# Attention's value projection in two pairs of seven block products, feature blocks turned in two portions, and the inverse norm turned behind the values

## The chip, the cores and the metric

The kernel runs on one core of one Trainium2 chip. The metric is the device time of one execution in microseconds (us), as the median of several runs. Engines are named as in the profile: PE is TensorE's matrix multiplication, PEld its loading of the stationary operand, DVE is VectorE, ACT ScalarE, POOL GpSimd, SP SyncE, which issues most DMAs. L181 means line 181 of the kernel before.

## What is computed

A two-layer decoder trunk on 256 tokens with 2048 features, all in 32-bit floats. Layer 0 mixes by two recurrent groups and layer 1 by attention; each layer ends in an MLP with 8192 hidden features. What the change touches is layer 1's projection and what stands beside it:

```python
def rms_norm(x, gain):
    xf = x.astype(F32)
    y = xf * lax.rsqrt(jnp.mean(xf * xf, axis=-1, keepdims=True) + NORM_EPS)
    return (y * gain.astype(F32)).astype(x.dtype)
...
def dilated_attention(h, positions, w_qkv, w_o):
    qkv = (h @ w_qkv).astype(F32).reshape(bsz, seq, 3, ATTN_HEADS, HEAD_DIM)
    q = partial_rope(qkv[:, :, 0], positions) * (HEAD_DIM ** -0.5)
    k = partial_rope(qkv[:, :, 1], positions)
    v = qkv[:, :, 2]
...
    out = (num / den).reshape(bsz, seq, D_MODEL).astype(h.dtype)
    return out @ w_o
...
def squared_relu_mlp(h, w1, w2):
    return jnp.square(jax.nn.relu(h @ w1)) @ w2
```

There are 16 heads of 128 features; rotary position coding turns the first 32 features of each query and key, by the sine and cosine of position times frequency.

## The kernel before

**Products.** Each 32-bit operand is split into a high part (rounded) and a low part (the rest), and a product is three matmuls: high by high, high by low, low by high. The activations lie in `bufa` (normalised input, turned to features by tokens) and `bufb` (attention's or the MLP's inner result), with high parts in the first 256 columns of each of 16 feature blocks and low parts in the next 256. The residual stream lies in `xall`/`xres` (two token blocks of 128 by 2048 features).

**Weights** stream from memory in units of 128x2048 (1 MB). `units` (L64, L80 to L88) is the list of all of them in order of use. `unit` (L170) hands out the next and calls `fetch` (L108), which runs some two units ahead: a DMA from SP into `raw`, then `split` makes the high part on ACT (L102) and the low part on DVE (L103). There are three buffers of each. Queries, keys and plain values are split in two steps of 1024 columns.

**Seven products for eight.** The MLP's weights go in pairs: two groups of 512 output columns (n0 and n0 + 1) by 16 feature blocks, of which the first eight (four and four, in the order of PAIRED) are paired: two token blocks by two halves of the paired features by two column groups are eight block products of 12 matmuls, and are got from seven, on sums of operands. `combine` (L124) makes the weights' sums: two adds of 128x2048 on DVE (L130) and an accumulating DMA on POOL (L142, into t1), and a third sum by DVE or, for the matrices in T4_DMA (L965), by a second POOL DMA (L148). Those of the activations are the forms in `formx` and `formh`: `combos` and `part_forms` (L591 to L600). `blocks` (L648) runs one pair in the order of ORDERS (L961 to L964), for w2: a, t1, n7, t2, c, n6, t3, d, n2, t4, n3, where n are the plain units of the other eight feature blocks. Four PSUM banks serve: beta for a, t2, t3, t4 and the sum (0, 1), alpha for t1, c and (1, 0), gamma for d and (0, 0), delta for (1, 1); the numbers are column group and token block. A plain unit n6 or n7 works on token block 1 first (into delta), then on token block 0 (into alpha). A bank that is used again must have been read out: `events` say by what, after each product, and `final` after each sum.

**Order on the engines.** Matmuls and turns made through `mm` (L180) and `turn` (L183) keep the order of the program on PE. For the other engines a scheduler orders instructions when the program is built, by priorities: `stream()` and `urgent()` raise those of the weights' stream and of the short work on results. That order is fixed in the built program; each engine works through its own in turn.

**Around the change.** The last MLP of layer 0 ends with `second` (L750): its `to_x` (L754) adds each finished bank to the residual on DVE, and `Norm.add` squares it on ACT with the sum kept (L291). When a feature block of 512 is complete, `to_features` (L614) queues its turning: four turns of 128x128 into PSUM, twice (L184), then the gain and the split into `bufa` (ACT L235, DVE L236). The queue is emptied by `flush` (L188), eight turns in one go. After that, `rstd` (L310) makes the inverse root of the mean square on DVE: one reduction (L295), one scaling (L296), and eleven operations on 128x2 (L317 to L322, three Newton steps), and `over_tokens` (L304) turns it to lie along tokens for the queries and keys (nr, L848). Since attention's input in `bufa` isn't yet divided by the root, values are multiplied by it when they leave PSUM (L348, ACT), and queries and keys after their product. `rotary` (L817) makes sine and cosine: a small DMA of the positions from POOL, some 16 operations of 32x256 on DVE, two Sin on ACT.

Attention goes in four groups of heads (L892 to L907): values of four heads (512 columns, 16 feature blocks, 96 matmuls of 128x512 per token block pair), then for each head `scores` (query and key projection, rope, softmax, turning) and `mix` (L885, weights by values, split into `bufb`). The last group has its values behind its scores. Then w_o's projection (`out_project`, L639) with residual, norm and turning, and the MLP of layer 1.

Of the kernel before, what the change touches and what calls it, by code (L numbers as in the profile page):

```python
# [20 lines left out]
P = 128  # L21
# [20 lines left out]
def trunk_kernel(ctx, tc, x, xtok, cols, tab, masks, pos, fin, w_in, w_gate, w_out, w_qkv, w_o, w1, w2, out):  # L42
# [28 lines left out]
    def plan2(src, i):  # L71
        for what, u in ORDERS[src is w2]:
            units.append((src, None if u is None else i + u, what, i))
# [7 lines left out]
    for layer in range(2):  # L81
        if layer:
            units.extend((w_qkv, i) for i in (0, 1, 3, 2, *range(4, 48)))
            plan(w_o, 16)
        for q in range(4):
            for src in (w1, w2):
                for n in range(0, 4, 2):
                    plan2(src, layer * 64 + q * 16 + 4 * n)  # L88
# [35 lines left out]
    def combine(u, src, i, what, i0):  # L124
# [7 lines left out]
        if what == "a":  # L132
            load("t1", i0 + 4, pair)
            load("a", i)
            held["s"] = pair.tile([P, 2048], F32, name="s")
            add("s", "a", "t1")
        elif what in ("n", "d"):
            load(what, i)
# [5 lines left out]
        if ahead == ("t4",) and src not in T4_DMA(w1, w2):  # L144
            add("s", "s", "d")
        made[u] = Weights(held[{"t1": "s", "t2": "s", "t3": "t1", "t4": "s"}.get(what, what)])
        if what == "c" and src in T4_DMA(w1, w2):
            nc.gpsimd.dma_start(held["s"], src[i0 + 1], accum_op=OP.add)  # L148
# [37 lines left out]
    later = []  # L186

    def flush(due=None):  # L188
        todo = later[:due]
        del later[:due]  # L190
        for f in todo:
            f()

# [110 lines left out]
    def over_tokens(r):  # L304
        p = psc.tile([P, 512], F32, name="pt", bufs=1)
        for j in range(2):
            T.transpose(p[:, j * P:j * P + P], r[:, j:j + 1].to_broadcast([P, P]), ident)
        return p[:, :S]
# [15 lines left out]
    def tokens(src, i0, mov, kgs=(0, 1, 2, 3), by_k=False):  # L324
        ks = PAIRED if src is w2 else range(KB)
        ps = [pmm.tile([P, 512], F32, name="p") for _ in range(2)]
        for g in kgs:
# [12 lines left out]
            flush()  # L340
# [10 lines left out]
    def project(src, i, mov, acc=None):  # L351
# [3 lines left out]
        if later:  # L355
            cross(p, w, jobs[:8], "h")
            flush()
            cross(p, w, jobs[8:12], "h")
            cross(p, w, jobs[:12], "l")
            jobs = jobs[12:]  # L360
# [226 lines left out]
    def open_pairs(layer):  # L587
        pool_ = pairs.enter_context(tc.tile_pool(name=f"pair{layer}", bufs=1))
        return pool_, [pool_.tile([P, 4, 2, 512], F32R, name=n) for n in ("formx", "formh")]
# [12 lines left out]
    pair, (formx, formh) = open_pairs(0)  # L602
# [11 lines left out]
    def to_features(n, gname, forms=None):  # L614
        def work():
            with urgent():
                for half in range(2):
                    p = psc.tile([P, 2, S], F32, name="pl", bufs=2)
                    for j in range(2):
                        for i in range(2):  # L620
                            k = 4 * n + 2 * half + i
                            turn(p[:, i, j * P:j * P + P], xres[:, j, k * P:k * P + P])
                    k = 4 * n + 2 * half
                    if forms is None:
                        for i in range(2):
# [22 lines left out]
    def blocks(src, i0, n0, mov, forms, events, final, soon=False):  # L648
# [6 lines left out]
        beta = psc.tile([P, 512], F32, name="po" if n0 else "pd", bufs=1)  # L655
# [55 lines left out]
    def first(i0, n0, soon):  # L711
# [23 lines left out]
        def final(n, j, bank):  # L735
            with urgent():
# [5 lines left out]
                else:  # L742
# [5 lines left out]
                                             "t3": u3}, final, soon)  # L748
# [24 lines left out]
    def mlp(layer, nrm, nxt, gname):  # L773
# [9 lines left out]
        r2n = tmp.tile([P, 2], F32, name="r2n", bufs=2)  # L783
# [3 lines left out]
        for q in range(4):  # L787
            ends = nxt if q == 3 else None

            def done(n):  # L790
                if ends is None:
                    return
                if gname:
                    to_features(n, gname)
# [6 lines left out]
            for n in (0, 2):  # L801
                first(layer * 64 + q * 16, n, q + n == 0)
# [43 lines left out]
    rt = rstd(nx1)  # L846
    rs = tmp.tile([P, S], F32, name="nr", bufs=1)
    A.copy(rs, over_tokens(rt))  # L848
# [9 lines left out]
    def scores(u0):  # L858
# [9 lines left out]
        s = wk.tile([P, 384], F32, name="as", bufs=3)  # L868
# [12 lines left out]
        st = wk.tile([P, 384], F32, name="pT", bufs=5)  # L881
# [3 lines left out]
    def mix(hd, st, vg, bank="po", bufs=1):  # L885
        vs = slice((hd % 4) * P, (hd % 4) * P + P)
# [78 lines left out]
T4_DMA = lambda w1, w2: (w1,)  # L965
# [32 lines left out]
def _layout(a):  # L998
# [30 lines left out]
    q_, k_, v_ = feat(wq[:, :2048]), feat(wq[:, 2048:4096]), toks(wq[:, 4096:])  # L1029
    w_qkv = []  # L1030
    for g in range(4):
        if g < 3:
            w_qkv.append(v_[4 * g:4 * g + 4])
        for h in range(4 * g, 4 * g + 4):
            w_qkv += [q_[h:h + 1], k_[h:h + 1]]
    w_qkv.append(v_[12:])
# [33 lines left out]
```

## Time and profile before

| what | value |
|---|---|
| median of 3 runs | 2167.29 us (2167.05 to 2167.54) |
| the profiled execution | 2166.9 us |
| its span in the profile | 2165.1 us |
| granted TensorE clock, mean | 0.998 |
| instructions in the profile | 27716 |
| weight splits: high 128x1024 and 128x2048, ACT (L102), in all | 486 + 96 operations, 689.3 + 183.7 us |
| DVE adds of weights 128x2048 (L130) `s<-s,raw` | 48, mean 2282 ns |
| weights by DMA from POOL into t (L142) | 32, median 8.7 us from issue to landing |

The span is the stretch that the profiler sees; what lies around it is 1.8 us. "Busy" of an engine is the time in which it had an instruction running; "idle before" is the time an engine waited ahead of an instruction, with what ended the wait. A chain line gives the start, the length and the instructions of a stretch that set the end.

### The profile page before, as it was taken

How to read it: one execution, taken by the hardware profiler on the slowest of the kernel's cores; microseconds unless marked ns; L12 is line 12 of the kernel's file. 1: busy time of each engine (PE TensorE's matmuls, PEld its weight loads, DVE VectorE, ACT ScalarE, POOL GpSimd, SP SyncE). 2: the span in 40 equal slices, each digit the busy share in tenths (PEclk: the TensorE clock that was granted, in tenths of full speed). 3: DMA queues.
4: the chain of work that ended last, by engine and by line, in shares of the span. 5: the costliest groups of instructions: out<-in, count | busy, mean ns of one | idle time of the engine just before them, and what ended most of it. 6: DMA issues, size and time to landing. Idle time of an engine off the chain costs nothing.

```text
span 2165.1 us, 27716 instructions
## 1 busy us (share of the span) xinstructions
PE 2146.9 (99%) x11044; PEld 1833.8 (85%) x11044; DVE 1792.2 (83%) x2094; ACT 1254.1 (58%) x1413; POOL 44.7 (2%) x57
## 2 busy tenths in 40 slices
PE   9999999999999999999999999999999999999997
PEld 8999998888888888888788888888888888888886
DVE  7776787789889889889877768667998998898897
ACT  7444485566466566466554544456655755755764
POOL 0000000000000000000000000000000000000000
PEclk9999999999999999999999999999999999999999
DMA  8444445587777687687664554557768777777873
GB/s 319 156 156 164 150 157 212 182 244 246 227 237 257 222 247 235 233 252 233 201 208 166 185 172 161 192 181 227 236 221 261 237 227 238 251 233 224 264 239 129
DMA packets 65857, 464.68 MB, mean 215 GB/s; under 512 B 7344, under 2 KB 8112, under 8 KB 10304
## 3 DMA queue, kind: packets, MB, share of 16 engines
q1 hardware_dynamic: 58176, 410.89, 53.2%
q0 software_dynamic: 7264, 51.42, 12.8%
q8 instruction: 87, 1.43, 0.3%
q10 hardware_dynamic: 288, 0.61, 0.1%
q14 instruction: 42, 0.34, 0.0%
HBM read 460.78 MB, written 2.10 MB: 214 GB/s over the span
## 4 chain that ended last, share of the span: by engine, by line
PE 95%; DVE 2%; ACT 1%; DMA 1%; issue 1%; SPq 0%; DVEq 0%; ACTq 0%
PE p L181 67%; PE po L181 12%; PE pd L181 11%; PE pl L184 2%; DVE lo L103 1%; PE pl L476 1%; ACT hi L102 0%; DMA raw<-in_w 0%; PE pl L867 0%; PE po L888 0%; DVE xall L754 0%; DMA xall<-in_x 0%; PE pd L880 0%; PE pd L460 0%; PE pl L866 0%
## 5 line engine op out<-in xcount | busy, mean ns | idle before, releaser
L102 ACT CAST hi<-raw 128x1024 fp32r<-128x1024 f32 (+2 forms) x486 | 689.3, 1443 | 563.0 <-PE p L181 372.7
L103 DVE TENSOR_TENSOR lo<-raw,hi 128x1024 fp32r<-128x1024 f32 (+2 forms) x486 | 822.2, 1708 | 223.1 <-ACT hi L102 205.4
L181 PE MATMUL p<-hi,bufb 128*128 128x512 f32 x1408 | 448.6, 390 | 2.1 <-DVE xall L754 2.0
L181 PE MATMUL p<-hi,bufa 128*128 128x512 f32 x1280 | 411.4, 392 | 0.8 <-ACT hi L102 0.8
L181 PE MATMUL p<-bufa,hi 128*128 128x256 f32 (+1 forms) x1792 | 364.9, 317 | 0.1
L181 PEld LDWEIGHTS p<-hi,bufb 128*128 128x128 f32 x1408 | 264.3, 188 | 60.1 <-DVE xall L754 5.5
L181 PEld LDWEIGHTS p<-bufa,hi 128*128 128x128 f32 x1792 | 294.5, 190 | 18.9 <-DVE hz L418 0.3
L181 PEld LDWEIGHTS p<-hi,bufa 128*128 128x128 f32 x1280 | 240.4, 188 | 53.0 <-DVE y L718 2.4
L181 PE MATMUL p<-lo,bufb 128*128 128x512 f32 x704 | 274.2, 389 | 1.2 <-DVE lo L103 1.2
L181 PE MATMUL p<-bufa,lo 128*128 128x256 f32 x1152 | 255.5, 287 | 0.0
L181 PE MATMUL p<-lo,bufa 128*128 128x512 f32 x640 | 250.6, 392 | 2.2 <-DVE lo L103 2.1
L103 DVE TENSOR_TENSOR lo<-s,hi 128x2048 fp32r<-128x2048 f32 x96 | 219.4, 2285 | 18.4 <-ACT hi L102 16.5
L102 ACT CAST hi<-s 128x2048 fp32r<-128x2048 f32 x96 | 183.7, 1913 | 48.3 <-PE po L181 21.8
L181 PEld LDWEIGHTS p<-bufa,lo 128*128 128x128 f32 x1152 | 189.3, 191 | 2.6
L181 PEld LDWEIGHTS p<-lo,bufb 128*128 128x128 f32 x704 | 132.2, 188 | 28.4 <-DVE lo L103 1.6
L181 PEld LDWEIGHTS p<-lo,bufa 128*128 128x128 f32 x640 | 120.2, 188 | 28.1 <-DVE lo L103 4.3
L130 DVE TENSOR_TENSOR s<-s,raw 128x2048 f32<-128x2048 f32 x48 | 109.5, 2282 | 1.3 <-DMA raw<-in_w 1.3
L181 PE MATMUL po<-hi,bufa 128*128 128x512 f32 x256 | 84.8, 392 | 0.0
L181 PE MATMUL pd<-hi,bufa 128*128 128x512 f32 x256 | 84.8, 392 | 0.0
L181 PE MATMUL p<-hi,formx 128*128 128x512 f32 x256 | 84.0, 389 | 0.0
L181 PE MATMUL p<-hi,formh 128*128 128x512 f32 x256 | 84.0, 389 | 0.0
L181 PE MATMUL pd<-hi,bufb 128*128 128x512 f32 x256 | 83.0, 389 | 0.0
(281 smaller groups left out, 2754.9 us busy)
## 6 DMA issues: line engine op xcount, KB each, us to landing
raw<-in_w SPq DMA_DIRECT2D x224, 1024.0 KB, 5.1
raw<-in_w_qkv SPq DMA_DIRECT2D x48, 1024.0 KB, 4.8
raw<-in_w_in SPq DMA_DIRECT2D x46, 1024.0 KB, 4.9
t<-in_w SPq DMA_DIRECT2D x32, 1024.0 KB, 5.7
t<-in_w POOLq DMA_DIRECT2D x32, 1024.0 KB, 8.7
raw<-in_w_out SPq DMA_DIRECT2D x16, 1024.0 KB, 4.9
s<-in_w POOLq DMA_DIRECT2D x16, 1024.0 KB, 9.2
raw<-in_w_o SPq DMA_DIRECT2D x16, 1024.0 KB, 4.8
```

Of the source, the lines that this page charges most:

```text
L102: A.copy(h, w)
L103: V.tensor_tensor(l, w, h.bitcast(F32), OP.subtract)
L130: V.tensor_tensor(held[to], held[x], held[y], OP.add)
L181: chain[:] = [after(T.matmul(*args, **kw), chain)]
L184: chain[:] = [after(T.transpose(out_, in_, ident), chain)]
L476: T.matmul(pl[:, j], kq[:, js], halves(qp[:, js], c, True), start=True, stop=True)
```

## The change

Attention's values are projected in two pairs of 1024 columns (heads 0 to 7, heads 8 to 15), each by `blocks`, as the MLP's products are, and so on forms of the normalised input in feature blocks 0 to 7; the weights are laid out for it. Each pair's results leave PSUM through `put` (ACT, scaled by the root or its negative) and `add` (DVE, scaled and added). All of `rstd` comes ahead of the first pair, the turning of the root along tokens behind it (now in PE's written order), and `rotary` behind that. Heads go in the order: values of 0 to 7, heads 0 to 7, scores of heads 8 to 11, values of 8 to 15, mix of 8 to 11, heads 12 to 15.

A feature block is now turned in two portions of four turns, each from the list `turns`, one behind a unit; this holds for all three places where blocks are turned (after layer 0's mixers, after layer 0's MLP, after w_o). The buffers change too: `formx`, t1 and s move to a pool that stays for the whole program, so `values` can use them; the pair pool of layer 0's MLP ends before attention and attention's tiles take its room; rotary's tiles move into attention's pool (positions and angle share `ra` and `rb` with rope), vg has one buffer in place of two (each twice as large), as two for three, pT four for five, r2n one for two.

```diff
     def plan2(src, i):
-        for what, u in ORDERS[src is w2]:
+        for what, u in ORDERS[src is not w1]:
             units.append((src, None if u is None else i + u, what, i))
...
-            units.extend((w_qkv, i) for i in (0, 1, 3, 2, *range(4, 48)))
+            for v, heads in ((0, 24), (32, 8)):
+                plan2(w_qkv, v)
+                units.extend((w_qkv, v + 8 + i) for i in range(heads))
             plan(w_o, 16)
...
         if what == "a":
-            load("t1", i0 + 4, pair)
+            load("t1", i0 + 4, both)
             load("a", i)
-            held["s"] = pair.tile([P, 2048], F32, name="s")
+            held["s"] = both.tile([P, 2048], F32, name="s")
             add("s", "a", "t1")
...
             load("c", i0 + 5)
             nc.gpsimd.dma_start(held["t1"], src[i0 + 5], accum_op=OP.add)
             add("s", "s", "c")
-        if ahead == ("t4",) and src not in T4_DMA(w1, w2):
+        if ahead == ("t4",) and src not in T4_DMA(w1, w2, w_qkv):
             add("s", "s", "d")
         made[u] = Weights(held[{"t1": "s", "t2": "s", "t3": "t1", "t4": "s"}.get(what, what)])
-        if what == "c" and src in T4_DMA(w1, w2):
+        if what == "c" and src in T4_DMA(w1, w2, w_qkv):
             nc.gpsimd.dma_start(held["s"], src[i0 + 1], accum_op=OP.add)
...
-    later = []
...
+    def turn_one():
+        if turns:
+            turns.pop(0)()
...
-        ks = PAIRED if src is w2 else range(KB)
+        ks = range(KB)
...
-            flush()
+            turn_one()
...
-        if later:
-            cross(p, w, jobs[:8], "h")
-            flush()
-            cross(p, w, jobs[8:12], "h")
-            cross(p, w, jobs[:12], "l")
-            jobs = jobs[12:]
...
-        return pool_, [pool_.tile([P, 4, 2, 512], F32R, name=n) for n in ("formx", "formh")]
+        return pool_, pool_.tile([P, 4, 2, 512], F32R, name="formh")
...
-    pair, (formx, formh) = open_pairs(0)
+    both = ctx.enter_context(tc.tile_pool(name="both", bufs=1))
+    formx = both.tile([P, 4, 2, 512], F32R, name="formx")
+    pair, formh = open_pairs(0)
...
-        def work():
+        def work(half):
+            k = 4 * n + 2 * half
             with urgent():
-                for half in range(2):
-                    p = psc.tile([P, 2, S], F32, name="pl", bufs=2)
-                    for j in range(2):
-                        for i in range(2):
-                            k = 4 * n + 2 * half + i
-                            turn(p[:, i, j * P:j * P + P], xres[:, j, k * P:k * P + P])
-                    k = 4 * n + 2 * half
-                    if forms is None:
-                        for i in range(2):
-                            split_to(bufa[:, k + i], p[:, i], col(gname, k + i))
-                        continue
-                    z = pair.tile([P, 2, 2, P], F32, name="y21")
+                p = psc.tile([P, 2, S], F32, name="pl", bufs=2)
+                for j in range(2):
                     for i in range(2):
-                        A.activation(z[:, i], p[:, i].rearrange("p (j c) -> p j c", j=2), AF.Copy,
-                                     scale=col(gname, k + i))
-                    zs = z.rearrange("p i j c -> p i (j c)")
-                    split_to(bufa[:, k:k + 2], zs)
-                    a11, a21, a12, a22 = (z[:, i, j] for i in range(2) for j in range(2))
-                    combos(a22, a11, a21, a12, a11, a21, a12, a22)
-                    part_forms(forms, k // 2, 1, slice(0, 4), z.rearrange("p i j (one c) -> p one (i j) c", one=1))
-        later.append(work)
+                        turn(p[:, i, j * P:j * P + P], xres[:, j, (k + i) * P:(k + i) * P + P])
+                if forms is None:
+                    for i in range(2):
+                        split_to(bufa[:, k + i], p[:, i], col(gname, k + i))
+                    return
+                z = pair.tile([P, 2, 2, P], F32, name="y4" if half else "y21")
+                for i in range(2):
+                    A.activation(z[:, i], p[:, i].rearrange("p (j c) -> p j c", j=2), AF.Copy, scale=col(gname, k + i))
+                split_to(bufa[:, k:k + 2], z.rearrange("p i j c -> p i (j c)"))
+                a11, a21, a12, a22 = (z[:, i, j] for i in range(2) for j in range(2))
+                combos(a22, a11, a21, a12, a11, a21, a12, a22)
+                part_forms(forms, k // 2, 1, slice(0, 4), z.rearrange("p i j (one c) -> p one (i j) c", one=1))
+        turns.extend([lambda: work(0), lambda: work(1)])
...
+        beta = psc.tile([P, 512], F32, name="pt" if src is w_qkv and i0 else "po" if n0 else "pd", bufs=1)
...
-        for what, u in ORDERS[src is w2]:
+        for what, u in ORDERS[src is not w1]:
             w = unit(src, None if u is None else i0 + 4 * n0 + u)
+            due, ready = len(later), len(turns)
             if what != "n":
                 times(bank[what], w, side[what])
                 if what in events:
                     events[what](bank[what])
-                if what == "t1" and soon:
-                    flush()
-                continue
-            n, g = divmod(u, 4)
-            plains[n] += 1
-            due = len(later)
-            for j in (1, 0) if n else (0, 1):
-                times(sums[n, j], w, lambda i, j=j, g=g: plain(j, 4 * g + i))
-                if plains[n] == 2:
-                    final(n, j, sums[n, j])
-            flush(due)
+            else:
+                n, g = divmod(u, 4)
+                plains[n] += 1
+                for j in (1, 0) if n else (0, 1):
+                    times(sums[n, j], w, lambda i, j=j, g=g: plain(j, 4 * g + i))
+                    if plains[n] == 2:
+                        final(n, j, sums[n, j])
+                flush(due)
+            if ready:
+                turn_one()
 
...
-                    to_features(n, gname)
+                    to_features(n, gname, formx if n < 2 else None)
...
-    vgs = mixers.enter_context(tc.tile_pool(name="vgs1", bufs=2))
+    vgs = mixers.enter_context(tc.tile_pool(name="vgs1", bufs=1))
     wk = mixers.enter_context(tc.tile_pool(name="wk2", bufs=2))
-    rot = mixers.enter_context(tc.tile_pool(name="rot", bufs=1))
     angles = {}
     swap = [(i + 16) % 32 for i in range(32)]
 
     def rotary():
-        ppi = rot.tile([32, S], I32, name="ppi")
+        ppi = wk.tile([32, S], I32, name="ra", bufs=2)
         nc.gpsimd.dma_start(ppi, bass.AP(tensor=pos.tensor, offset=pos.offset, ap=[[0, 32], [1, S]]))
-        ang = rot.tile([32, S], F32, name="ang")
-        cosT = rot.tile([32, S], F32, name="cosT")
-        sinT = rot.tile([32, S], F32, name="sinT")
+        ang = wk.tile([32, S], F32, name="rb", bufs=2)
+        cosT = wk.tile([32, S], F32, name="cosT", bufs=1)
+        sinT = wk.tile([32, S], F32, name="sinT", bufs=1)
...
-    rt = rstd(nx1)
-    rs = tmp.tile([P, S], F32, name="nr", bufs=1)
-    A.copy(rs, over_tokens(rt))
...
-        s = wk.tile([P, 384], F32, name="as", bufs=3)
+        s = wk.tile([P, 384], F32, name="as", bufs=2)
...
-        st = wk.tile([P, 384], F32, name="pT", bufs=5)
+        st = wk.tile([P, 384], F32, name="pT", bufs=4)
...
-        vs = slice((hd % 4) * P, (hd % 4) * P + P)
+        vs = slice((hd % 8) * P, (hd % 8) * P + P)
...
-    pend = []
-    for g in range(4):
-        if g < 3:
-            vg = tokens_group(w_qkv, g * 12, rt, kgs=(0, 1, 2, 3) if g else (0, 1, 3, 2))
-        if not g:
-            rotary()
-        for hd in range(4 * g, 4 * g + 4):
-            u0 = g * 12 + (4 if g < 3 else 0) + (hd % 4) * 2
-            st = scores(u0)
-            if g < 3:
-                mix(hd, st, vg)
-            else:
-                pend.append(st)
-    vg = tokens_group(w_qkv, 44, rt)
-    for hd, bank in zip(range(12, 16), (("po", 1), ("pd", 1), ("pl", 2), ("pl", 2))):
-        mix(hd, pend[hd - 12], vg, *bank)
+    with urgent():
+        rt = rstd(nx1)
+        rtn = tmp.tile([P, 2], F32, name="rtn", bufs=1)
+        V.tensor_scalar(rtn, rt, -1.0, None, op0=OP.mult)
+
+    def values(i0):
+        v = vgs.tile([P, 2, 2, 512], F32, name="vg")
+
+        def put(n, j, r=rt):
+            def event(bank):
+                with urgent():
+                    A.activation(v[:, j, n], bank, AF.Copy, scale=r[:, j:j + 1])
+            return event
+
+        def add(n, j, bank, r=rt):
+            with urgent():
+                V.scalar_tensor_tensor(v[:, j, n], bank, r[:, j:j + 1], v[:, j, n], op0=OP.mult, op1=OP.add)
+
+        blocks(w_qkv, i0, 0, bufa, formx,
+               {"a": put(0, 0), "t1": put(1, 1), "t2": put(1, 0, rtn), "t3": lambda b: add(1, 1, b, rtn)},
+               lambda n, j, b: put(n, j)(b) if (n, j) == (0, 1) else add(n, j, b))
+        return v.rearrange("p j n c -> p j (n c)")
+
+    vg = values(0)
+    rs = tmp.tile([P, S], F32, name="nr", bufs=1)
+    with urgent():
+        A.copy(rs, over_tokens(rt, turn))
+    rotary()
+    for hd in range(8):
+        mix(hd, scores(8 + 2 * hd), vg)
+    pend = [scores(24 + 2 * i) for i in range(4)]
+    vg = values(32)
+    for i, bank in enumerate((("po", 1), ("pd", 1), ("pl", 2), ("pl", 2))):
+        mix(8 + i, pend[i], vg, *bank)
+    for i in range(4):
+        mix(12 + i, scores(40 + 2 * i), vg)
 
     mixers.close()
-    pair, (formx, formh) = open_pairs(1)
+    pair, formh = open_pairs(1)
...
-T4_DMA = lambda w1, w2: (w1,)
+T4_DMA = lambda w1, w2, w_qkv: (w1, w_qkv)
```

Here `both` is the lasting pool. The weights' layout on the host follows the new order of units, with the values' feature blocks in the order of PAIRED.

More of the change, by code (lines that the diff above doesn't have):

```diff
@@ L184, in turn @@
         chain[:] = [after(T.transpose(out_, in_, ident), chain)]
-    later = []
+    later, turns = [], []
     def flush(due=None):
@@ L302, in inv_mean, with over_tokens @@
             return m
-    def over_tokens(r):
+    def over_tokens(r, turn=lambda o, i: T.transpose(o, i, ident)):
         p = psc.tile([P, 512], F32, name="pt", bufs=1)
         for j in range(2):
-            T.transpose(p[:, j * P:j * P + P], r[:, j:j + 1].to_broadcast([P, P]), ident)
+            turn(p[:, j * P:j * P + P], r[:, j:j + 1].to_broadcast([P, P]))
         return p[:, :S]
@@ L646, in trunk_kernel, with blocks @@
     nrm = out_project(w_out, "nmlp0", (2, 3, 0, 1))
-    def blocks(src, i0, n0, mov, forms, events, final, soon=False):
+    def blocks(src, i0, n0, mov, forms, events, final):
         plain = lambda j, k: (mov[:, k, j * P:j * P + P], mov[:, k, S + j * P:S + j * P + P])
@@ L654, in blocks @@
         alpha, delta, gamma = (pmm.tile([P, 512], F32, name="p") for _ in range(3))
-        beta = psc.tile([P, 512], F32, name="po" if n0 else "pd", bufs=1)
+        beta = psc.tile([P, 512], F32, name="pt" if src is w_qkv and i0 else "po" if n0 else "pd", bufs=1)
         bank = {"a": beta, "t1": alpha, "t2": beta, "c": alpha, "t3": beta, "d": gamma, "t4": beta}
@@ L709, in to_h, with first @@
         later.append(work)
-    def first(i0, n0, soon):
+    def first(i0, n0):
         keep, tiles = {}, {}
@@ L747, in first @@
         blocks(w1, i0, n0, bufa, formx, {"a": hold("y1", A.copy, 2), "t1": hold("y4", V.tensor_copy), "t2": hold("y2", A.copy),
-                                             "t3": u3}, final, soon)
+                                             "t3": u3}, final)
     def second(i0, n0, nrm, r2, r2n, done, gains):
@@ L782, in mlp @@
         r2 = nrm.inv_mean()
-        r2n = tmp.tile([P, 2], F32, name="r2n", bufs=2)
+        r2n = tmp.tile([P, 2], F32, name="r2n", bufs=1)
         V.tensor_scalar(r2n, r2, -1.0, None, op0=OP.mult)
@@ L801, in mlp @@
             for n in (0, 2):
-                first(layer * 64 + q * 16, n, q + n == 0)
+                first(layer * 64 + q * 16, n)
             for n in (0, 2):
@@ L1028, in _layout @@
     wq = n(a["attn_w_qkv"][0])
[L1029 to L1036, printed above, removed]
+    q_, k_, v_ = feat(wq[:, :2048]), feat(wq[:, 2048:4096]), toks(wq[:, 4096:], PAIRED)
+    qk = [w[h:h + 1] for h in range(16) for w in (q_, k_)]
+    w_qkv = [v_[:8], *qk[:24], v_[8:], *qk[24:]]
     w1 = np.concatenate([toks(n(w)[:, q * 2048:q * 2048 + 2048], PAIRED) for w in a["mlp_w1"] for q in range(4)])
```

## The prediction

> **What bounds the kernel now.** I read the page's busy times first, then its chain of work that ended last, then the waits of PE alone, then the timelines of PE and DVE where the first layer's MLP hands over to attention (1050 to 1118 us), because that is where the change puts its work.
>
> ```profile
> PE 2146.9 (99%) x11044; PEld 1833.8 (85%) x11044; DVE 1792.2 (83%) x2094; ACT 1254.1 (58%) x1413; POOL 44.7 (2%) x57
> ...
> PE 95%; DVE 2%; ACT 1%; DMA 1%; issue 1%; SPq 0%; DVEq 0%; ACTq 0%
> ```
>
> PE is the bound nearly everywhere: busy 99% of the span, and 95% of the chain. So a matmul taken away is worth its pace, unless a new wait gives it back. All waits of PE, by what ended them (us in total, times, longest):
>
> ```profile
> PE p L181 <- DVE lo L103: 3.3, 4, 1.2
> PE p L181 <- DVE xall L754: 2.0, 2, 1.3
> PE po L246 <- DVE xp L528: 1.1, 1, 1.1
> ```
>
> Few and short; none is in attention. The pace of a 128x512 matmul is read from the chain, where the 96 matmuls of one values group stand as one line (start, us):
>
> ```profile
> 1422.03 21.78 PE p L181 x96
> ```
>
> 21.78 / 96 = 0.2269 us each (a single record shows 0.39 us, since records overlap). Two of the waits are in the last w2 block of layer 0, and after the second come eight turns of a feature block in one go (start, us, what ran, and in brackets what it had waited for):
>
> ```profile
> 1062.64 0.50 PE L181 MATMUL p<-lo,bufb 128*128 128x512 f32 x1 [1.17 <-DVE lo L103]
> ...
> 1066.17 0.50 PE L181 MATMUL p<-hi,bufb 128*128 128x512 f32 x1 [0.71 <-DVE xall L754]
> ...
> 1069.02 1.03 PE L184 MATMUL pl<-tab__181,xall 128*128 128x128 f32 x8
> ```
>
> The next matmul starts at 1069.81, so eight turns take 0.79 us and four about 0.4. DVE, 83% busy over all, is the late engine here: both waits are for it.
>
> **What goes.** A values pair (1024 columns, 16 feature blocks) is 192 matmuls of 128x512 before and 180 after: 7 block products of 12, and 8 plain ones of 12 for the half of the inputs that is not paired. In order, the built programs differ by exactly 24 such matmuls on PE; turns and all else are as many. 24 x 0.2269 = **-5.45 us**. DVE and ACT get 11 weight splits for 8 in each pair, two adds of 128x2048 (2.28 us each by L130's row), and the forms of feature blocks 0 to 7; SP gets no more than its 1 MB loads, POOL four accumulating DMAs. Inside the values that is hidden: a pair is 180 x 0.2269 = 40.8 us of PE against 11 splits (lo 128x2048: 2.285 us) + 2 adds = 29.7 us of DVE. Most of it is beside PE, except in four places.
>
> **Place 1: the first values block.** Call E the end of the last w2 matmul. PE then runs product a (12 matmuls, 2.72 us), four turns, t1 (2.72), four turns, and the plain unit n7. The last to_x, 0.74 us behind an add of 2.28 us on DVE, is done about E + 2.9; the four turns after a need it, so a PE wait of 0.2 there, and n7's half for token block 1 ends at 2.72 + 0.2 + 0.4 + 2.72 + 0.4 + 2.72, about E + 9.1. Its other half accumulates into the bank that t1 wrote and that the change now evacuates through put(1,1), ACT, scaled by the inverse root of the mean square. Before, values were left in PSUM for 96 matmuls (21.8 us) before anything wanted that root. So the question is when the root is ready. Before, the chain ran like this on DVE (from the reduction of the squares to the last of eleven small operations):
>
> ```profile
> 1105.10 0.14 DVE L295 TENSOR_REDUCE nm<-ss 128x2 f32<-128x8 f32 x1
> 1105.21 0.28 DVE L838 TENSOR_SCALAR cosT<-cosT 32x256 f32<-32x256 f32 x1
> ...
> 1107.50 1.23 DVE L103 TENSOR_TENSOR lo<-raw,hi 128x1024 fp32r<-128x1024 f32 x1 [0.42 <-ACT hi L102]
> 1108.65 0.15 DVE L321 SCALAR_TENSOR_TENSOR rs<-rs,nm 128x2 f32<-128x2 f32 x1
> ...
> 1111.74 0.15 DVE L322 SCALAR_TENSOR_TENSOR nr<-rs,nr 128x2 f32<-128x2 f32 x1
> ```
>
> 6.8 us, mixed with rotary operations and splits, with nobody waiting. In the changed program's DVE order the same chain stands behind the last to_x so: position cast (0.27), lo split of n7 (2.2 start to start), a rotary step (0.25), lo split of t2 (2.2), reduce, one gain split (0.4), a rotary step, mean (together 1.0): E + 8.9. Then lo split of c (2.2): E + 11.1. Then eleven small operations left for the root, with fourteen others among them: three gain splits (0.40 start to start), four rotary 32x256 SCALAR_TENSOR_TENSOR (0.33), seven shorter ones (0.21); the small ones follow at 0.08 to 0.2, 0.12 in the mean. That is 1.2 + 1.3 + 1.5 + 1.3 = 5.3 us, root at E + 16.4. On ACT the Sin table load (1.28 by its row) and two Sin stand ahead of put; they wait for cosT and sinT, that come among the last of these DVE operations; then put(0,0) and put(1,1), 0.69 each by the 128x512 row of L348: about E + 17.7. PE wait: 17.7 - 9.1 = **+8.6 us**. What is queued behind the waiting matmul is all of PE. From below: with the small operations wholly within the others' time, 8.6 - 1.3 = 7.3. From above: the position cast waits for a DMA which POOL issues behind the accumulation of t1, and these took 8.7 us to land in the page's row; up to 2.4 more, 11.
>
> **Place 2: the last w2 block of layer 0.** Turns of block 0 now come in two portions, the first behind product a. They need the to_x of the block before, that stands behind an add which waited for its DMA (1057.44, 1.30 us of waiting); it is done some 5 us after this block's start, against 2.7 for a: a wait of 2.0, and 0.5 later at the turn of block 3. They take the place of the 2.2 us seen above (1.17 + 0.71 and their after-effects). Net **+0.3**; from -1 (the old stalls go and the new ones are smaller) to +2 (DVE has 5.6 us of form work more here and falls further back).
>
> **Place 3: the second values block.** The same half of n7 waits for put(1,1), which stands on ACT behind an exponential of the last pending head, a few tenths to 1.2 us: **+0.6** (0 to 1.2).
>
> **Place 4: before the output projection.** in the built order the two matmuls of mix(15) stand among w_o's, right ahead of the 81st, the first that reads head 15. Nothing is between them to cover mix's split into bufb: a copy on ACT that stands behind two hi splits, then a subtraction on DVE behind lo splits. Its two operations alone take 0.37 and 0.42 us (the 128x256 rows of L232 and L233); a split of 128x2048 in the way, up to 1.9 or 2.3, would cover all but a part of itself. I take **+1.15** (0.6 to 2). Before, the four mixes had w_o's first 80 matmuls, 18 us, behind them.
>
> Turning by fours costs nothing by itself: the change of kind on PE was 0 to 0.1 us in the rows around 1069.
>
> **Sum**, against the profiled execution (2166.9 us, span 2165.1): -5.45 + 8.6 + 0.3 + 0.6 + 1.15 = +5.2, so 2172.1. The median of the runs is 2167.29, 0.4 above that execution: **2172.5 us**.
>
> **The clock.** The 24 warm-up matmuls at the start (L246) show two paces in their records: the first ones 421 ns long and 0.213 us apart until 4.3 us into the span, the later ones 275 ns and 0.112 apart. The half pace cost 15 x 0.101 = 1.5 us. Waits up to 1.5 us later in the kernel left the pace at once as it was. A wait of 8.6 us lies between: nothing to 1.5 us. The profile's granted clock is 1.00 even in the first 4 us, so that row cannot tell. I put nothing in the forecast and 1.5 in a rival. [...]
>
> **Rivals.** (a) *The clock falls in the wait.* Then 2172.5 + 1.5 = 2174.0. For it: the start of the span. Against it: no wait so far did it, but none was over 1.5 us. (b) *DVE falls behind further*: the cast waits for its DMA, and the form operations of four more halves (each four of 128x128 at 0.21 and two of 128x512 at 0.6, by the rows of the same lines in layer 0, less the gain splits that they replace) delay to_x; 2172.5 + 2.4 + 1.7 = 2176.6. For it: DVE already ends both waits there; against it: ACT and the buffers limit DVE too, and DVE idles 1 us here and there before 1092. (c) *The root is in time*: not slower. If the root's operations run as soon as the last square is there (E + 3.7; thirteen operations of 0.2 us: E + 6.3; the two puts done at E + 7.7), the first half of n7 covers it and place 1 costs nothing: 2172.5 - 8.6 = 2163.9, and 2161.9 if places 2 to 4 cost nothing too. It decides at E + 9.1. For it: the edit marks these operations as urgent. Against: they stand in the built order behind three splits of 2.2 us, which cannot be overtaken on one engine. (d) That the change leaves out what it says is excluded: the matmuls are counted.
>
> **Chances.** Forecast 0.45, (a) 0.27, (b) 0.13, (c) 0.11, something else 0.04. Faster or slower counts from 0.2% = 4.3 us, about what a measurement of this kernel can tell: under 2163.0, over 2171.6. The forecast's own low end (7.3, -1 and 0.6 in place of 8.6, 0.3 and 1.15) is 2169.4, so a quarter of it is "same"; (a) is slower but for a tenth, (b) slower, (c) half faster and half same. Faster 0.06, same 0.20, slower 0.74. The range of eight in ten: from 2168.5 (the low end less a little, without (c)) to 2177.5 (upper part of (b)).
>
> **What would show it.** PE's waits: one of 7 to 11 us at a matmul with bufa about 9 us after the last w2 matmul, released by ACT's put; the small operations of the root on DVE 11 to 16 us after E; 24 matmuls fewer; two waits of 2.0 and 0.5 for to_x in the last w2 block; about 1 us ahead of w_o's block 15. After the long wait, matmuls 0.45 us apart for 3 us would show (a). Wrong if no wait over 3 us stands there, or if DVE's order on the chip lets the root out earlier.

## The result and the profile after

The changed kernel takes 2175.97 us (median of 6 runs, 2174.42 to 2176.86) against 2167.68 us of the kernel before on the same chip: ratio 1.0038, 95% interval 1.0025 to 1.0051, 8.3 us slower. The profiled execution took 2176.81 us, 9.9 more than the one before; its span is 2174.7 us, 9.6 more. The page's busy times:

```profile
PE 2147.9 (99%) x11020; PEld 1833.0 (84%) x11020; DVE 1821.7 (84%) x2113; ACT 1268.0 (58%) x1411; POOL 48.2 (2%) x61
```

24 matmuls fewer on PE (11020 for 11044), and yet PE is not busy for less time. Its waits say where a part went (us in total, times, longest):

```profile
PE p L183 <- ACT vg L897: 8.3, 1, 8.3
PE pl L186 <- DVE xall L752: 1.9, 1, 1.9
PE p L183 <- DVE lo L105: 1.8, 3, 0.8
PE p L183 <- DVE xall L752: 1.4, 1, 1.4
...
PE p L183 <- ACT bufb L238: 0.5, 1, 0.5
```

The first line is new and the longest wait of the kernel: put (L897) in the first values block. The second is the turn behind product a in the last w2 block of layer 0; the two waits seen there before are gone. The timeline of DVE shows how late the root is. E, the end of the last w2 matmul, is 1103.3 here, as the next block's first matmul starts at 1103.27:

```profile
1109.03 2.27 DVE L105 TENSOR_TENSOR lo<-s,hi 128x2048 fp32r<-128x2048 f32 x1
1111.23 0.14 DVE L301 TENSOR_REDUCE nm<-ss 128x2 f32<-128x8 f32 x1
...
1111.96 2.27 DVE L105 TENSOR_TENSOR lo<-raw,hi 128x2048 fp32r<-128x2048 f32 x1
...
1116.66 0.14 DVE L327 SCALAR_TENSOR_TENSOR rs<-rs,nm 128x2 f32<-128x2 f32 x1
1116.77 0.41 DVE L830 SCALAR_TENSOR_TENSOR rb<-cosT,rb 32x256 f32<-32x256 f32 x1
...
1119.33 0.16 DVE L328 SCALAR_TENSOR_TENSOR nr<-rs,nr 128x2 f32<-128x2 f32 x1
```

The reduction at E + 8.0, the root at E + 16.2, with splits and rotary operations among its own. ACT takes it up within 0.2 us, as its timeline in the same stretch shows (the two puts):

```profile
1119.68 0.66 ACT L897 ACTIVATE vg<-pd,nr 128x512 f32<-128x512 f32 x1
1120.25 0.66 ACT L897 ACTIVATE vg<-p,nr 128x512 f32<-128x512 f32 x1
```

And PE follows; its timeline from the waiting matmul on:

```profile
1120.97 0.80 PE L183 MATMUL p<-hi,bufa 128*128 128x512 f32 x1 [8.29 <-ACT vg L897]
1121.56 0.63 PE L183 MATMUL p<-lo,bufa 128*128 128x512 f32 x1
1121.99 1.06 PE L183 MATMUL p<-hi,bufa 128*128 128x512 f32 x2
1122.84 0.63 PE L183 MATMUL p<-lo,bufa 128*128 128x512 f32 x1
...
1126.67 0.40 PE L183 MATMUL pd<-lo,formx 128*128 128x512 f32 x1
```

Single matmuls are 0.63 us long here for 0.39, and start 0.43 us apart for 0.227, until 1126.67. The table by stretches of time has the granted clock in its fourth column (start:end length, PE busy and matmuls, clock, DMA share, GB/s):

```profile
1058.00:1061.00 3.00, 1.60 (x9) 1.00 0.38 158
1061.00:1062.00 1.00, 0.52 (x3) 0.90 0.00 0
1062.00:1065.00 3.00, 3.00 (x8) 0.50 0.29 35
1065.00:1066.00 1.00, 1.00 (x5) 0.90 0.52 180
...
1116.00:1117.00 1.00, 0.00 (x0) 0.71 0.90 188
1117.00:1126.00 9.00, 5.03 (x12) 0.50 0.49 159
1126.00:1127.00 1.00, 1.00 (x5) 0.67 0.00 0
```

A clock of 0.90 over a microsecond is 0.2 us at half. So it was at half from 1061.8 to 1065.2, after the turn's wait, and from 1116.4 to 1126.7, in and after the long one. The trace's own record of the clock, from which this column is made, has the same four times.

**Account of the 9.6 us**, from the same matmuls in both timelines: +0.8 up to the last w2 block (0.5 of it from the start to 300 us, most of the rest by 530 us; the first product starts at 6.20 for 5.44); +1.7 in the last w2 block (E is 1103.27 for 1100.74); +6.9 from E to the first turn in w_o (1430.4 for 1421.0, less the 2.5 before it); +0.2 after. The 6.9 is -5.45 for 24 matmuls, about +8.4 for the wait with what follows directly, 13 matmuls at half pace (+2.7), +0.9 for mix of head 15 ahead of w_o, and a rest of 0.3.

The 0.5 of the start goes with the clock; that the edit has no part in it is an estimate, from the warm-up matmuls being the same 24. The clock record shows full rate from 4.34 us on before and only from 7.08 in the change, and the 24 warm-up matmuls take 5.49 us there for 4.50. (The column shows 1.00 ahead of the record's first entry too, so it can't tell this.)

### The profile page after: what moved, and what is told of

Same layout as the page of the kernel before. It is cut to its first block, busy times and chain, and to the rows that moved or that the text cites. A ratio compares the mean times of both kernels' runs of the same rounds, so it can differ in the third digit from the quotient of the medians.

```text
span 2174.7 us, 27696 instructions
## 1 busy us (share of the span) xinstructions
PE 2147.9 (99%) x11020; PEld 1833.0 (84%) x11020; DVE 1821.7 (84%) x2113; ACT 1268.0 (58%) x1411; POOL 48.2 (2%) x61
## 5 line engine op out<-in xcount | busy, mean ns | idle before, releaser
L104 ACT CAST hi<-raw 128x2048 fp32r<-128x2048 f32 (+2 forms) x468 | 683.9, 1484 | 571.7 <-PE p L183 369.3
L105 DVE TENSOR_TENSOR lo<-raw,hi 128x2048 fp32r<-128x2048 f32 (+2 forms) x468 | 816.4, 1759 | 209.3 <-ACT hi L104 194.2
L183 PE MATMUL p<-hi,bufa 128*128 128x512 f32 x1136 | 368.2, 393 | 9.1 <-ACT vg L897 8.3
L183 PEld LDWEIGHTS p<-hi,bufa 128*128 128x128 f32 x1136 | 214.7, 189 | 57.0 <-ACT vg L897 8.7
L105 DVE TENSOR_TENSOR lo<-s,hi 128x2048 fp32r<-128x2048 f32 x102 | 233.2, 2286 | 16.9 <-ACT hi L104 14.8
L183 PE MATMUL p<-lo,bufa 128*128 128x512 f32 x568 | 222.8, 392 | 1.8 <-DVE lo L105 1.8
L104 ACT CAST hi<-s 128x2048 fp32r<-128x2048 f32 x102 | 195.1, 1912 | 48.0 <-PE po L183 22.0
L183 PEld LDWEIGHTS p<-lo,bufa 128*128 128x128 f32 x568 | 107.4, 189 | 24.7 <-DVE lo L105 3.1
L183 PE MATMUL p<-hi,formx 128*128 128x512 f32 x288 | 95.6, 392 | 0.0
L105 DVE TENSOR_TENSOR lo<-t,hi 128x2048 fp32r<-128x2048 f32 x34 | 77.8, 2287 | 13.2 <-ACT hi L104 13.2
```

The source lines that it names most:

```text
L104: A.copy(h, w)
L105: V.tensor_tensor(l, w, h.bitcast(F32), OP.subtract)
L183: chain[:] = [after(T.matmul(*args, **kw), chain)]
```

## Experiments

**Values without the root (e1).** The same mathematics, with the root applied where the softmax weights leave PSUM:

```diff
-        A.copy(st, pt)
+        A.activation(st[:, :S], pt[:, :S], AF.Copy, scale=rt[:, 0:1])
+        A.activation(st[:, S:], pt[:, S:], AF.Copy, scale=rt[:, 1:2])
...
-        def put(n, j, r=rt):
+        def put(n, j, r=1.0):
...
-                    A.activation(v[:, j, n], bank, AF.Copy, scale=r[:, j:j + 1])
+                    A.activation(v[:, j, n], bank, AF.Copy, scale=r)
...
-        rtn = tmp.tile([P, 2], F32, name="rtn", bufs=1)
-        V.tensor_scalar(rtn, rt, -1.0, None, op0=OP.mult)
```

> The changed kernel, but values leave PSUM unscaled (puts and adds with 1 and -1), and the inverse root is applied to the softmax weights when they are copied out of PSUM after their turning (two ACT operations a head in place of one); same mathematics. Theory (the wait is for the root alone, and the half pace after it comes from the wait): the 8.3 us wait in the first values block and the 13 matmuls at 0.43 us after it (2.7 us) both go, 11 us less than the changed kernel: some 3 us below the kernel before, 2164.5. Rival (the block itself is too much for DVE, and the wait only moves to a split or a form): a wait of 3 us or more by DVE lo or formx in that block, and a time above 2168.

Measured 2172.33 us, ratio to before 1.0022 (1.0013 to 1.0032). The wait for put is gone, nothing took its place in the values block, and no matmul between 1040 and 1440 us goes at half pace (the mean granted clock is 0.999, for 0.995 in the change); that much is the theory. But the time is 8 us above the forecast, and neither side foresaw where: e1 loses evenly, in both MLPs, which the edit doesn't touch. Two of the groups of matmuls on forms, in e1 (after the name: busy us in all, mean ns of one):

```profile
L183 PE MATMUL p<-lo,formx 128*128 128x512 f32 x144 | 56.9, 395 | 0.0
L183 PE MATMUL po<-hi,formx 128*128 128x512 f32 x128 | 43.4, 400 | 0.0
```

The same two groups in the changed kernel:

```profile
L183 PE MATMUL p<-lo,formx 128*128 128x512 f32 x144 | 56.0, 389 | 0.0
L183 PE MATMUL po<-hi,formx 128*128 128x512 f32 x128 | 42.7, 395 | 0.0
```

In starts it is clearer: matmuls with formx or formh follow each other after 232.7 ns in the mean in e1, 226.9 in the changed kernel (some 1590 of each counted from 425 to 2140 us); those with bufa or bufb after 227 in both. Dropping the little tile rtn had moved the forms by 32 bytes. e9 and e11 follow this up.

**The w2 portions a unit later (e5).**

```diff
-            if ready:
+            if ready and not (src is w2 and what == "a"):
                 turn_one()
```

> The changed kernel, with the portions in the w2 blocks turned behind t1 and n7 and not behind a and t1. Theory (the 1.9 us wait in the last w2 block is for the last add to the residual, which is done 5 us after the block's start, and the half pace after it follows from the wait): that wait and the half pace of 1061.5 to 1065.3 go, 3.5 to 4 us less than the changed kernel, 2172; the wait of the first values block stays at 8 to 8.6 us. Rival (DVE is late by its form work, and the wait only moves to lo splits as before): 1 to 2 us less at most, with waits of 1 us and more for DVE lo in that block.

Measured 2177.25 us, 1.0045 (1.0032 to 1.0059): not faster than the change. Its timeline of PE shows where the waits are now:

```profile
1063.52 0.50 PE L183 MATMUL p<-lo,bufb 128*128 128x512 f32 x1 [0.85 <-DVE lo L105]
1067.25 0.50 PE L183 MATMUL p<-hi,bufb 128*128 128x512 f32 x1 [0.95 <-DVE xall L752]
1107.57 0.69 PE L186 MATMUL pl<-tab__181,xall 128*128 128x128 f32 x2 [2.64 <-DVE xall L752]
1122.95 0.79 PE L183 MATMUL p<-hi,bufa 128*128 128x512 f32 x1 [7.59 <-ACT vg L897]
```

The two waits of the kernel before are back; that much is the rival's mechanism. The new one of 2.6 us, at the turn in the values block, has another cause, which DVE's timeline shows:

```profile
1104.37 0.28 DVE L820 CAST rb<-ra 32x256 f32<-32x256 int32 x1 [2.46 <-DMA ra<-in_pos]
...
1106.78 0.73 DVE L752 SCALAR_TENSOR_TENSOR xall<-po,nm,xall 128x512 f32<-128x512 f32 x1
```

In this built order the position cast stands ahead of the add of weights (between these lines) and of the last to_x (L752), where it stands behind both in the changed kernel. Its DMA, issued by POOL right behind the accumulation of t1, took 8.5 us to land, and DVE stood idle for it 2.46 us. The turn follows that to_x. So e5 moved more than the portions, and it doesn't tell what turning a unit later alone would give.

**Both (e6).** e1 and e5 together.

> Both edits together: values unscaled with the root in the softmax weights, and the portions of the w2 blocks turned one unit later. Theory: both gains add, 15 us less than the changed kernel, about 2161 and 0.3% under the kernel before; no wait of PE over 1 us between 1040 and 1160 us, and the granted clock is 1.00 there. Rival: something else in the first values block is late next (a put on ACT behind hi splits, a form on DVE), a wait of 2 us or more with its half pace, and 2164 or more.

Measured 2176.18 us, 1.0039 (1.0027 to 1.0052), with the forms 32 bytes off as in e1. The wait for put is gone, but three waits for DVE stand as in e5 (0.5, 0.9 and 2.9 us), the last with half pace behind it (the mean granted clock is 0.997, for 0.999 in e1): the rival's figure, though not with a put or a form. As in e5, the cast stands ahead of the last to_x and waits for its DMA, here 2.75 us.

**Turns in portions alone (e3)**: the kernel before with `turn_one`, the two halves of to_features and the loop of `blocks` from the change's diff; values, rotary and root as before.

> One part alone: the kernel before, with feature blocks turned in two portions as in the change (values, rotary and the root as before; no forms for attention's input). Theory (the loss in the last w2 block comes from turning behind a): a wait of about 2 us there in place of the two of before, the half pace after it, +1.5 to +2 us against the kernel before. Rival (it comes from the form work that DVE has more in the change): no wait over 1.5 us there, within 0.5 us of the kernel before.

Measured 2167.15 us, 1.0000 (0.9991 to 1.0009). The rival's figure, but not for its reason: the wait of the theory is there, 1.57 us at the first turn (1061.05) in place of the two of before, yet no half pace followed (clock 1.00 from 1056 to 1066), and without it the portions cost nothing.

**Filling the long wait (e2).** 32 extra matmuls of 128x512, whose result isn't used, ahead of the waiting one:

```diff
                 for j in (1, 0) if n else (0, 1):
+                    if src is w_qkv and not i0 and what == "n" and u == 7 and not j:
+                        idle = psc.tile([P, 512], F32, name="pt", bufs=1)
+                        for _ in range(32):
+                            mm(idle, bufa[:, 0, :P], w.hi[:, :512], start=True, stop=True)
                     times(sums[n, j], w, lambda i, j=j, g=g: plain(j, 4 * g + i))
```

> The changed kernel, with 32 extra matmuls of 128x512 into an unused bank put in PE's order where it waits in the first values block (their results aren't used; 32 x 0.227 = 7.3 us). Theory (the half pace comes from PE being idle): the wait falls to about 1 us, the granted clock stays at 1.00 there and the matmuls after it go at 0.227 us: 2.7 us less than the changed kernel although 32 matmuls are added, some 2173. Rival (the half pace has another cause, such as the load of the other engines): the pace after the wait stays 0.43 and the time is that of the changed kernel.

Measured 2172.44 us, 1.0025 (1.0015 to 1.0035): 3.5 us less than the changed kernel with 32 matmuls more. In the table of stretches:

```profile
1112.00:1118.00 6.00, 5.74 (x26) 1.00 0.93 227
1118.00:1120.00 2.00, 0.71 (x3) 1.00 0.74 311
1120.00:1124.00 4.00, 4.00 (x20) 1.00 0.00 0
```

The clock stays at 1.00, the put comes no earlier, and 1.5 us of the wait are left. So the half pace of 1117 to 1126 us, at 0.50 in the change, comes from PE being idle there. In this execution the 1.8 us wait at the turn had no half pace either (clock 1.00 from 1056 to 1068), so the 3.5 us may hold more than the 2.7 of the long wait.

**Filling the short wait (e8).** 8 such matmuls ahead of the first turn in the w2 block:

```diff
+            if ready and src is w2 and what == "a":
+                idle = psc.tile([P, 512], F32, name="pt", bufs=1)
+                for _ in range(8):
+                    mm(idle, mov[:, 0, :P], w.hi[:, :512], start=True, stop=True)
             if ready:
                 turn_one()
```

> The changed kernel, with 8 extra matmuls of 128x512 (1.8 us, results not used) ahead of the turns behind product a in those w2 blocks of layer 0 and 1 where turns are waiting, that is in the last block of layer 0. Theory: the wait of 1.9 us there is filled, the clock stays at 1.00, and 1.7 to 1.9 us go against the changed kernel. Rival (a wait of 2 us is too short for that, the half pace is a coincidence): no change, within 0.5 us.

Measured 2175.23 us, 1.0037 (1.0023 to 1.0052). The clock is 1.00 from 1058 to 1066, but the time is only 0.7 us below that of the change, within the spread of both: the put's wait is 8.8 us here for 8.3. This alone doesn't settle how much the short wait's half pace costs in the median.

**Rotary ahead of the first MLP (e4)**: `rotary()` is called ahead of `mlp(0, ...)`, with cosT and sinT in the lasting pool.

> The changed kernel, with rotary made ahead of the first MLP, so that none of its operations stand among those of the root; the root's place and the scaled evacuation stay. Theory (the root is late for the operations that stand among its own on DVE, some 3 us of them rotary, and for the weight splits ahead): the wait in the first values block falls from 8.3 to 5 or 5.5 us, its half pace stays or falls by one window, 3 to 5 us less than the changed kernel. Rival (the splits ahead alone set it): the wait stays at 7.5 us or more.

Measured 2170.8 us, 1.0017 (1.0008 to 1.0026), 5.2 us less than the change. The wait falls as foreseen:

```profile
PE p L183 <- ACT vg L898: 5.2, 1, 5.2
```

and the clock is at half for 6.8 us (1113.0 to 1119.9), where it was 10.2: 3.4 less, as much as the change's whole stretch from 1061.8 to 1065.2. 3.1 us of the wait went with rotary; what is left are the splits ahead and the chain itself.

**e1 with rtn kept (e9).** The edit of e1, but rtn is still computed, so formx is at address 167744 again, as in the change.

> e1 again (values unscaled, root in the softmax weights), but the small tile rtn, which e1 had dropped, is kept. In e1 formx and formh had moved by 32 bytes with it (address 167712 for 167744, no longer a multiple of 64), and its matmuls with formx or formh as the stationary operand stood 0.233 us apart for 0.227 in both MLPs. Theory (the address makes these matmuls slower, and the root's wait is gone as in e1): the pace is 0.227 again everywhere, some 9 us less than e1, 2163, 0.2% under the kernel before. Rival (the slower pace comes from the values' edit itself or from that placement of the program): it stays, and 2172.

Measured **2163.6 us**, 0.9985 (0.9976 to 0.9994): below the kernel before. PE's waits, with none for put:

```profile
PE p L183 <- DVE lo L105: 1.7, 3, 0.8
PE pl L186 <- DVE xall L752: 1.7, 1, 1.7
PE p L183 <- DVE xall L752: 1.4, 1, 1.4
```

The forms' matmuls are back at 226.9 ns; no half pace from 1100 to 1130 us (matmuls 0.39 us long). 8.7 us less than e1, and 12.4 less than the change.

**The address alone (e11)**: the changed kernel with 32 bytes ahead of formx.

```diff
+    pad = both.tile([P, 8], F32, name="pad")
+    V.memset(pad, 0.0)
     formx = both.tile([P, 4, 2, 512], F32R, name="formx")
```

> The changed kernel with an empty tile of 32 bytes ahead of formx, so that formx and formh stand 32 bytes off a multiple of 64; nothing else. Theory (address): matmuls on forms 0.233 us apart, 9 to 10 us more than the changed kernel, 2185. Rival (address without effect): 2176, pace 0.227.

Measured 2185.87 us, 1.0087 (1.0074 to 1.0101): 9.9 more than the change, forms 233.0 ns apart; the tiles behind formx move by 32 bytes with it. Its row for the first of the groups shown of e1:

```profile
L183 PE MATMUL p<-lo,formx 128*128 128x512 f32 x144 | 56.9, 395 | 0.0
```

**Form sums on POOL (e10)**: in e9, the four subtractions and additions of `combos` of attention's portions go to `nc.gpsimd`.

> e9 with the four sums of operands of attention's four form portions (128x128 each) on POOL in place of DVE. Theory (what is left is one wait of 1.6 to 1.9 us in the last w2 block for the add to the residual, which DVE reaches late): DVE has 3.4 us less there, but the add waits behind its own DMA too, so 0 to 1 us less than e9. Rival (POOL's operations are so slow, or hold up DVE, that forms come late): a wait for formx or POOL of 1 us or more in the first values block, and slower than e9.

Measured 2166.36 us, 0.9997 (0.9988 to 1.0007), 2.8 slower than e9. POOL takes 0.5 to 1.6 us for each of them against 0.29 on DVE:

```profile
L599 POOL TENSOR_TENSOR y<-y 128x128 f32<-128x128 f32 x4 | 6.3, 1576 | 0.3
L600 POOL TENSOR_TENSOR y<-y 128x128 f32<-128x128 f32 x4 | 6.2, 1541 | 0.3
```

Waits for the residual add grew from 1.7 to 2.9 us (two), the longest (2.34) with half pace behind it in its profile (matmuls 0.43 us apart). Slower, as the rival has it, but the wait it named (for forms or POOL) isn't the one that grew. DVE reaches the residual add of the first wait at 1060.64, in e9 at 1059.78. The add of weights ahead of it starts 0.46 us later, and an operation on formx (0.60) stands between the two, where e9 has a sum (0.20). Beside POOL's operations some of DVE's are longer than in e9 (`bufa<-y,bufa` 0.95 us for 0.68, a split 2.44 for 2.28); no run separates the two causes.

## Why the prediction was right or wrong

**Right: sign, cause and place; the size partly by luck.** The time lay in the range and was slower. But it is 3.5 us above the forecast, and above rival (a)'s 2174.0 too; the range reaches that far because of rival (b), which didn't happen. In the profiled executions the sum was +5.2 and the measured +9.6: the clock gave 2.7 and 1.4 that were not in it, the time up to the last w2 block 0.8, and the other terms together came out 0.5 too high. *What goes*: 24 matmuls, as counted. *Place 1*: a wait of 8.29 us where 8.6 was worked out; the root at E + 16.2 (16.4), put done at E + 17.6 (17.7), PE's first half of n7 done at E + 9.2 (9.1). That the root is the cause is shown: e1 and e9 take it away, and e4 shortens it by the rotary share. The working held because the built order was followed operation by operation, each at its start-to-start time, and not because the operations are slow; eleven small ones make 1.3 us, and the rest is what stands among them.

**Wrong size: the clock.** The step "I put nothing in the forecast and 1.5 in a rival" failed. Rival (a) is what happened, and larger: 2.7 us after the long wait, since the half pace lasted 5.7 us of work and not the 3.2 of the start (15 matmuls 0.213 us apart) that the 1.5 was worked out from. The clock record of the change has half rate for 3.41 us (1061.80 to 1065.21) and for 10.24 (1116.41 to 1126.65), and the table of e4 has it for 6.8. The wait's length alone doesn't give the cost: behind waits of 5.2 us (e4), 8.3 (the change) and 8.8 (e8) the work at half pace lasted 3.9, 5.7 and 4.3 us, so the longest wait hadn't the longest half pace. Half of that work is an estimate of the cost, 2.0 to 2.8; the forecast should have held some 2.3.

**Wrong: the half pace at a short wait.** In place 2 the wait came as forecast (1.88 for 2.0) with net +0.3, but 8 to 9 matmuls at half pace made it +1.7. The 0.5 forecast at the turn of block 3 didn't come. "Waits up to 1.5 us later in the kernel left the pace at once as it was" was true and the next length was not covered. At this turn the clock was at 0.50 from 1061.8 on behind the wait of 1.88 us in the change, and matmuls went 0.43 us apart behind the 2.34 of e10; behind the 2.64 in the values block of e5 the clock was 0.57 from 1108 to 1111. Behind 1.8 us at this turn in e2 and 1.57 in e3 it stayed at 1.00. What parts these cases isn't shown. As 1.8 and 1.88 lie so near to each other, the half pace may come in one run of the changed kernel and not in the next; that is an estimate.

**Smaller terms.** Place 3: nothing for 0.6, put in the second block came in time. Place 4: 0.46 us of wait at block 15 of w_o, 0.9 with the slower matmul after it, for 1.15. The start, +0.5, was not in the sum; it goes with full rate from 7.08 us on in place of 4.34, and nothing of the change stands there. The 0.3 between there and the last w2 block was not in it either, and no run explains it.

**Rival (b)** didn't happen in the change: DVE reached the position cast at E + 3.1 and waited 0.1 us, as its DMA had landed (5.6 us after its issue). Its first half happened in e5 and e6: the cast's wait for that DMA, 2.46 and 2.75 us where 2.4 was worked out. **Rival (c)** didn't happen, but e9 reaches its end by another way: the put no longer needs the root, and 2163.6 was measured where (c) worked out 2163.9. That they agree so closely is partly luck, since the start, place 3 and place 4 were each off by 0.2 to 0.7.

Open: how often the short wait brings half pace in the changed kernel, what turning a unit later gives with the cast in its old place, and how much of e10's delay is POOL's and how much the order on DVE. Moving mix of head 15 away from w_o (0.9 us) wasn't tried.

## What to carry to other kernels

When a result must leave a buffer before the next product, ask what scale its way out needs and when that scale is ready on its engine's built order; a factor per row can often be applied later, where it has long been there. A wait of PE can cost more than its length: here 8 to 9 matmuls at half pace came behind one of 1.88 us (net +1.7 for the forecast +0.3) and 5.7 us of work at half pace behind one of 8.29 (2.7), and filling the long one with matmuls whose result isn't used took that part away (e2, clock 1.00). An edit to one engine's order can move others in the built program: look for what else moved (the cast in e5 and e6) before reading its time. And after an edit that drops or adds a small tile, look at the addresses of the big ones: here 32 bytes weighed more than the whole change (9.9 us in e11, for 8.3).

## What was not expected of the hardware

Matmuls of 128x512 with formx or formh as the stationary operand came 233 ns apart for 227, some 2.6% slower, with formx at address 167712 (e1) and with 32 bytes put ahead of it in the change (e11), against the same matmuls with formx at 167744 (e9, the change). No run tells why, or at which other addresses it is so. PEld's records of the loads for lo by formx are 188 ns in the mean in all four, so they don't show where the 6 ns go. In the change the clock fell to half at 1061.8 though PE had been busy for 1.5 us of the 3.4 before (1058.4 to 1061.8), and not only in the wait of 8.29 us; and it stayed at half until 1126.65 though PE was busy for 2.2 us of 3.4 from 1119.8 to 1123.2.
